# Cached keys of an encoder step: staged through a DRAM scratch into float32r tiles and transposed in that type

## Chip, cores and metric

The kernel runs on one core of a Trainium2 chip. The metric is the time of one execution on the device, in microseconds (us). TensorE (PE) multiplies matrices and transposes tiles; each of its products or transpositions is a pair of instructions, a weight load (listed as PEld) and a MATMUL that streams the other operand. VectorE (DVE), ScalarE (ACT) and GpSimd (POOL) do the rest of the arithmetic. SyncE (SP) issues the DMAs, in one queue and in order; 16 DMA engines carry them out.

## What is computed

One inference step of a four-layer encoder: 256 prompt tokens and 8 streams of 16 sample tokens, model width 2048, everything in float32. Every layer makes one projection of the normalised tokens, runs a token mixer with 12 heads beside a cross-attention with 4 heads into 256 memory tokens, multiplies both by a SiLU gate and projects back. Layers 0 and 3 use mixer A (sliding window), layer 1 mixer B (latent attention), layer 2 mixer C (chunk band). Cut to the attention with cached keys, for which the change matters:

```python
def attend(q, k, v, bias, valid, sink):
    ...
    s = jnp.einsum("bqhgd,bkhd->bhgqk", qg, k, ...) * (d ** -0.5)
    ...
    o = jnp.einsum("bhgqk,bkhd->bqhgd", p.astype(v.dtype), v)

# sample tokens, per stream: the cached rows stand ahead of the new ones
# A: cache_a_k, 128 rows, 4 heads of 128     C: cache_c_k, 512 rows, 12 heads of 128
# B: cache_b_ckv, 512 rows of 256, and cache_b_krope, 512 rows of 64
# cross-attention: cache_mem_k, 256 rows, 4 heads of 128, in every layer
```

The caches hold keys with one row per token, while a score product on TensorE needs the head's 128 dimensions on the partitions. So every 128x128 block of a cached key is transposed before it is used.

## The kernel before

The work is written in program order and a scheduler of the framework lays it out on the engines, so that products of the next projection fill the time between the steps of an attention. Memory keys and values of the prompt come first (`memory_kv`: 4 layers, two projections `pn_m` each), then the four layers. A layer projects (`proj_nat`, tiles `pn_...`, output columns 512 or 320 wide), mixes, makes the gate (`proj_tr`, `pt_g`, 384 columns wide) and projects back (`pt_o`; in the last layer `pn_o`). All these products run on weights that `w_split` loads from DRAM in pieces of 512 KB (`raw_...`, L144) and splits into two float32r halves: ScalarE rounds (`whi_...`), VectorE takes the rest (`wlo_...`). The pool `rawp` holds three such pieces. A second pool, `cchp`, holds five tiles of 512 KB for cached keys and values; while the memory keys are made, every other group of four rows of weight blocks uses it too (`ahead`).

A cached key is loaded straight from the input into a float32 tile of `cchp`: `kxs` for the memory keys (L450), `ak` for mixer A (L557), `kccs` for C (L711), `ckvkn` for the latent rows of B (L984); the rotary rows `krokn` (L986) go to a slot of `xtp`. `tr` (L101 to L103) transposes one block of 128 rows into a PSUM bank: the block is the weight operand, the identity `identr` streams past it. Four blocks fill a bank (`mkpsxs`, `mkpsp`, `ktpas`, `ktpcs`, `ctkn`, `krkn`), and VectorE or ScalarE copies it to SBUF (`kcT...`, `mkT...`, or the halves `chkn` and `clkn`). Banks of the kind `pt` are two, those of the kinds `s`, `o` and `ht` one each. The prompt's own memory keys take another way: they are written to a DRAM scratch (`memk_s`) and read back as `mk`.

One transposition in the kernel already works on float32r: line 1041 in `sample_b`, tile `rtbs`, 32 blocks of 64 columns.

Of the kernel before, what the change touches and what calls it, by code (L numbers as in the profile page):

```python
# [18 lines left out]
P = 128  # L19
# [40 lines left out]
def encoder_step(ctx: ExitStack, tc: tile.TileContext, ins: dict, outs: list, layers=(0, 1, 2, 3)):  # L60
# [25 lines left out]
    def cache_half(nm, q=2):  # L86
        return cchp.tile([P, q, 1024 // q], F32, tag="cch", name=nm)

    def mm(out, lhsT, rhs, start=True, stop=True):
        return nc.tensor.matmul(out, lhsT=lhsT, rhs=rhs, start=start, stop=stop)  # L90
# [43 lines left out]

    def w_split(nm, src, ncols, gcol=None, ahead=False):
# [24 lines left out]

    def proj_nat(nm, xt, w, ncols, ts=(0, 1, 2), gcol=None, first=0, ahead=False):
        nk = len(xt)
        ps = [pjb(f"pn_{nm}{t}") for t in ts]
        kstep = min(4, nk)
        order = [(first + i) % nk for i in range(0, nk, kstep)]
        for kg in order:
            wt = w_split(f"{nm}{kg}", w[kg * P:(kg + kstep) * P], ncols,
                         None if gcol is None else gcol[:, kg:kg + kstep], ahead and (kg // kstep) % 2 == 1)
            for i, t in enumerate(ts):
                for kk in range(kstep):  # L170
                    k = kg + kk
                    xh = xt[k][:, 0, t * P:(t + 1) * P]
                    xl = xt[k][:, 1, t * P:(t + 1) * P]
                    wh, wl = wt[kk]
                    mm(ps[i][:, :ncols], xh, wh, k == order[0], False)
                    mm(ps[i][:, :ncols], xh, wl, False, False)
                    mm(ps[i][:, :ncols], xl, wh, False, k == order[-1] + kstep - 1)
        return ps

    def proj_tr(nm, xt, w, first=0):  # L180
# [97 lines left out]
    def head_scale(n, f, g=None, nt=NT):  # L278
# [3 lines left out]
        if g is not None:  # L282
            nc.gpsimd.tensor_tensor(out=v, in0=v, in1=g.unsqueeze(1).to_broadcast([P, nh, HD]), op=ALU.mult)

    def memory_kv():
        xt = []
# [134 lines left out]
    def cross(l, xqT, oT, mul=False):  # L421
        mk, mv = cache_half(f"mk{l}"), cache_half(f"mv{l}")
        nc.sync.dma_start(out=mk, in_=memk_s[l].rearrange("(t p) d -> p t d", p=P))
        nc.sync.dma_start(out=mv, in_=memv_s[l].rearrange("(t p) d -> p t d", p=P))

        def kT(nm, mk):
            res = []
# [12 lines left out]

        mkT = kT(f"p{l}", mk)
        for h in range(4):
            attn_full(f"x{l}{h}", xqT[:, h, 0:256], mkT[h], mv[:, 0, h * P:(h + 1) * P],
                      mv[:, 1, h * P:(h + 1) * P], oT[:, H + h, 0:256], mul)
        for b2 in range(NB // 2):
            nm = f"xs{l}{b2}"
            mk, mv = ([cache_half(f"{t}{nm}{i}") for i in range(2)] for t in "kv")
            for t_, src in ((mk, "cache_mem_k"), (mv, "cache_mem_v")):
                for i in range(2):
                    nc.sync.dma_start(out=t_[i], in_=I[src][l, 2 * b2 + i].rearrange("(t p) h d -> p t (h d)", p=P))  # L450
            s = atb(f"s_{nm}", "s")
            for i in range(2):
                mkT = kT(f"{nm}{i}", mk[i])
                c0 = SP0 + DS * (2 * b2 + i)
# [96 lines left out]
    def sample_a(l, j, p2, qs, kT, vn, sink_r, oT):  # L551
        kvs = slice(2 * p2, 2 * p2 + 2)
        kcs, vcs = [], []
        for i in range(2):
            for ts, src in ((kcs, "cache_a_k"), (vcs, "cache_a_v")):
                ts.append(cache_half(f"a{src[-1]}{l}{p2}{i}", 4))
                nc.sync.dma_start(out=ts[i].rearrange("p b (h d) -> p b h d", h=2),  # L557
                                  in_=I[src][j, 4 * i:4 * i + 4, :, kvs, :].rearrange("b p h d -> p b h d"))
        for b2 in range(4):
            nm = f"as{l}{p2}{b2}"  # L560
            ps = atb(f"ktp{nm}", "s")
            for i in range(4):
                tr(ps[:, i * P:(i + 1) * P], kcs[b2 // 2][:, 2 * (b2 % 2) + i // 2, (i % 2) * P:(i % 2 + 1) * P])
            kcT = sm.tile([P, 512], F32, tag="kcT", name=f"kcT{nm}", bufs=4)
# [103 lines left out]
    def layer_c(l, xt, rx, xres, last):  # L668
# [3 lines left out]
        for g in range(3):  # L672
# [32 lines left out]
            for b in range(NB):  # L705
                nm = f"cs{g}{b}"
                kc, vc = [], []
                for ts, src in ((kc, "cache_c_k"), (vc, "cache_c_v")):
                    for i in range(2):
                        ts.append(cache_half(f"{src[-1]}c{nm}{i}"))  # L710
                        nc.sync.dma_start(out=ts[i], in_=I[src][0, b, 256 * i:256 * i + 256, hs, :].rearrange("(t p) h d -> p t (h d)", p=P))  # L711
# [57 lines left out]
    def layer_b(l, xt, rx, xres, last):  # L769
# [73 lines left out]
        def two_heads(qc):  # L843
# [137 lines left out]
        def key_norms(b):  # L981
            nm = f"kn{b}"
            raw = cache_half(f"ckv{nm}", 4)
            nc.sync.dma_start(out=raw, in_=I["cache_b_ckv"][0, b].rearrange("(t p) d -> p t d", p=P))  # L984
            kro = slot(f"kro{nm}")[:, 0:256].rearrange("p (t d) -> p t d", t=4)
            nc.sync.dma_start(out=kro, in_=I["cache_b_krope"][0, b].rearrange("(t p) d -> p t d", p=P))  # L986
            ss = tiny.tile([P, 48], F32, tag="kss", name=f"ss{nm}", bufs=2)
# [7 lines left out]
            for a in range(2):  # L995
                ps = atb(f"ct{nm}{a}", "ht")
                for kt in range(4):
                    tr(ps[:, kt * P:(kt + 1) * P], raw[:, kt, a * P:(a + 1) * P])
                nc.scalar.copy(ch[:, a, :], ps)
# [3 lines left out]
            for kt in range(4):  # L1003
                tr(ps[:64, kt * P:(kt + 1) * P], kro[:, kt, :])
            krT = sm.tile([P, 512], F32, tag="kcT", name=f"krT{nm}", bufs=4)
# [212 lines left out]

    setting = setup()
    memory_kv()  # L1220
    next(setting)
    xt = []
# [9 lines left out]
    for l in layers:  # L1232
        last = l == layers[-1]
        if l in (0, 3):
            xt, rx, xres = layer_a(l, l // 3, xt, rx, xres, last)
        elif l == 1:
            xt, rx, xres = layer_b(l, xt, rx, xres, last)
        else:
            xt, rx, xres = layer_c(l, xt, rx, xres, last)
# [33 lines left out]
```

## Time and profile before

| what | us |
|---|---|
| time before, median of 3 runs (2868.43 to 2872.82) | 2870.96 |
| the profiled execution, its own time | 2873.3 |
| its span, from the first to the last instruction | 2870.2 |
| PE busy | 2837.7 (99%) |
| PE weight loads busy | 2484.1 (87%) |
| VectorE busy | 1345.5 (47%) |
| ScalarE busy | 1322.9 (46%) |
| DMA engines busy | 47.6% of the span |

Durations of MATMULs overlap: the next begins before the end of the last has left the array. What one costs in a row of its kind is therefore the distance from its start to the start of the next, not its own duration; busy time is the union of the durations. "Idle before" is the time in which an engine had nothing running, with what ended it. The granted clock (PEclk) is a share of 2.4 GHz.

### The profile page before, as it was taken

What the parts mean: (1) busy time and instruction counts of PE and PEld (TensorE: products, weight loads), DVE (VectorE), ACT (ScalarE), POOL (GpSimd) and SP (SyncE); (2) the same over time, 40 slices, a digit from 0 to 9 for tenths busy, and PEclk for the clock granted to TensorE, in tenths of its full rate; (3) what the DMA queues carried; (4) which work ended last, traced back from release to release, by engine and by line L of the source; (5) the groups of instructions that cost most, each with busy time, mean ns of one, the idle gap of its engine ahead of it and who ended that gap; (6) DMA issues with size and microseconds to landing.
All of it is one profiled execution on the core that took longest, in us unless ns stands there. A gap on an engine that the chain in (4) does not pass through costs nothing.

```text
span 2870.2 us, 43881 instructions
## 1 busy us (share of the span) xinstructions
PE 2837.7 (99%) x17106; PEld 2484.1 (87%) x17106; DVE 1345.5 (47%) x2569; ACT 1322.9 (46%) x2819; POOL 425.7 (15%) x437
## 2 busy tenths in 40 slices
PE   8999999999999999999999999999999999999999
PEld 6867888999989987888898878788989988789987
DVE  5544345553435456565534434344545344445433
ACT  6655455443444366454434444444434344554332
POOL 1100111111100045333111101010101111011100
PEclk9999999999999999999999999999999999999999
DMA  7776453354444632000544465656566444533443
GB/s 255 249 264 211 158 173 117 125 186 152 143 138 118 191 92 73 16 19 26 162 161 139 138 199 193 222 178 239 180 233 230 151 136 132 195 114 100 133 157 128
DMA packets 314625, 446.79 MB, mean 156 GB/s; under 512 B 20629, under 2 KB 183462, under 8 KB 314418
## 3 DMA queue, kind: packets, MB, share of 16 engines
q1 hardware_dynamic: 314418, 444.00, 47.6%
q8 instruction: 134, 2.20, 0.3%
q14 instruction: 73, 0.60, 0.1%
HBM read 412.46 MB, written 34.69 MB: 156 GB/s over the span
## 4 chain that ended last, share of the span: by engine, by line
PE 96%; DMA 2%; DVE 1%; ACT 1%; SPq 0%; issue 0%; DVEq 0%; ACTq 0%
PE pt_g L90 19%; PE pt_o L90 14%; PE pn_aq L90 7%; PE kpkn L90 5%; PE pn_o L90 5%; PE pn_m L90 4%; PE pn_xq L90 4%; PE pn_cv L90 3%; PE pn_ck L90 3%; PE pn_cq L90 3%; PE pn_av L90 2%; PE pn_ak L90 2%; PE ktpcs L103 2%; PE s_bs L90 1%; PE pn_bqb L90 1%; PE pn_bq L90 1%
## 5 line engine op out<-in xcount | busy, mean ns | idle before, releaser
L90 PE MATMUL pt_g<-xt_x,whi_g 128*128 128x384 f32 x2048 | 532.4, 341 | 0.0
L90 PE MATMUL pt_o<-og,whi_o 128*128 128x384 f32 x1536 | 379.2, 334 | 0.0
L90 PEld LDWEIGHTS pt_g<-xt_x,whi_g 128*128 128x128 f32 x2048 | 367.3, 188 | 7.4 <-issue 4.9
L90 PE MATMUL pt_g<-xt_x,wlo_g 128*128 128x384 f32 x1024 | 342.9, 342 | 0.0
L150 DVE TENSOR_TENSOR wlo_o<-raw_o,whi_o 128x1024 fp32r<-128x1024 f32 x128 | 157.2, 1228 | 264.8 <-ACT whi_o L149 264.6
L90 PEld LDWEIGHTS pt_o<-og,whi_o 128*128 128x128 f32 x1536 | 276.1, 188 | 0.0
L149 ACT CAST whi_o<-raw_o 128x1024 fp32r<-128x1024 f32 x128 | 134.6, 1052 | 281.5 <-PE pt_o L90 147.5
L90 PE MATMUL pt_o<-og,wlo_o 128*128 128x384 f32 x768 | 245.7, 335 | 0.0
L150 DVE TENSOR_TENSOR wlo_g<-raw_g,whi_g 128x1024 fp32r<-128x1024 f32 x128 | 164.0, 1281 | 159.0 <-ACT whi_g L149 155.4
L149 ACT CAST whi_g<-raw_g 128x1024 fp32r<-128x1024 f32 x128 | 134.2, 1049 | 167.7 <-PE pt_g L90 142.9
L90 PEld LDWEIGHTS pt_g<-xt_x,wlo_g 128*128 128x128 f32 x1024 | 191.9, 188 | 5.4 <-issue 4.6
L90 PE MATMUL pn_aq<-whi_aq,xt_x 128*128 128x512 f32 x576 | 185.9, 398 | 0.0
L90 PE MATMUL pn_m<-whi_m,xt_m 128*128 128x512 f32 x512 | 161.6, 394 | 0.5 <-ACT whi_m L154 0.4
L90 PEld LDWEIGHTS pt_o<-og,wlo_o 128*128 128x128 f32 x768 | 143.2, 188 | 0.0
L90 PE MATMUL kpkn<-wk,chkn 128*128 128x384 f32 x512 | 133.7, 343 | 0.0
L155 DVE SCALAR_TENSOR_TENSOR wlo_m<-raw_m,gc_mem,whi_m 128x512 fp32r<-128x512 f32 x128 | 97.6, 804 | 75.7 <-ACT whi_m L154 75.7
L90 PEld LDWEIGHTS pn_aq<-whi_aq,xt_x 128*128 128x128 f32 x576 | 107.4, 188 | 22.5 <-issue 1.2
L90 PE MATMUL pn_xq<-whi_xq,xt_x 128*128 128x512 f32 x384 | 122.9, 397 | 0.5 <-ACT xt_x L214 0.5
L90 PE MATMUL pn_o<-whi_o,og 128*128 128x512 f32 x384 | 119.6, 391 | 0.0
L90 PE MATMUL pn_aq<-wlo_aq,xt_x 128*128 128x512 f32 x288 | 115.0, 401 | 0.0
L90 PEld LDWEIGHTS pn_m<-whi_m,xt_m 128*128 128x128 f32 x512 | 95.8, 189 | 21.2 <-ACT whi_m L154 1.1
L154 ACT ACTIVATE whi_m<-raw_m,gc_mem 128x512 fp32r<-128x512 f32 x128 | 85.8, 717 | 58.6 <-PE pn_m L90 58.2
(499 smaller groups left out, 5872.3 us busy)
## 6 DMA issues: line engine op xcount, KB each, us to landing
raw_o<-in_w_out_dram SPq DMA_DIRECT2D x128, 512.0 KB
raw_m<-in_w_mem_kv_dram SPq DMA_DIRECT2D x64, 512.0 KB
raw_g<-in_a_w_in_dram SPq DMA_DIRECT2D x64, 512.0 KB
raw_aq<-in_a_w_in_dram SPq DMA_DIRECT2D x48, 512.0 KB
kccs<-in_cache_c_k_dram SPq DMA_DIRECT2D x48, 512.0 KB
vccs<-in_cache_c_v_dram SPq DMA_DIRECT2D x48, 512.0 KB
kxs<-in_cache_mem_k_dram SPq DMA_DIRECT2D x32, 512.0 KB
vxs<-in_cache_mem_v_dram SPq DMA_DIRECT2D x32, 512.0 KB
```

The lines of the kernel that those rows point to most:

```text
L90: return nc.tensor.matmul(out, lhsT=lhsT, rhs=rhs, start=start, stop=stop)
L103: nc.tensor.transpose(out, in_, ident[:k, :k])
L149: nc.scalar.copy(hi[:, :, :ncols], r)
L150: nc.vector.tensor_tensor(lo[:, :, :ncols], r, hi[:, :, :ncols].bitcast(F32), ALU.subtract)
L154: nc.scalar.activation(hi[:, i, :ncols], r[:, i, :], AF.Copy, scale=g)
L155: nc.vector.scalar_tensor_tensor(lo[:, i, :ncols], r[:, i, :], g, hi[:, i, :ncols].bitcast(F32), ALU.mult, ALU.subtract)
```

## The change

Every cached key gets a second home in DRAM. `stage` makes a DRAM tile of the same shape as the later SBUF tile and puts the copy on a list; `move` takes copies from that list and issues them on SP, DRAM to DRAM, right behind a weight load (`issue_after`). `key_half` later loads the staged copy into a tile of `cchp` whose type is float32r (the DMA itself sees both sides as float32). `trr` transposes it with float32r on both sides of the transposition. The copies out of PSUM and the score products are untouched, and the cached values are loaded as before.

The copies are 104: 32 of memory keys, 8 of A, 48 of C, 8 of latent rows of B (512 KB each) and 8 of rotary rows (128 KB). Those for layer 0 are issued behind weight loads of `memory_kv` from its second layer on, those for layer 1's memory keys behind gate loads of layer 0, those for B, for C and for layer 2's memory keys behind gate loads of layer 1, the six `wkv` loads (four each) and the loads of rotary rows (three each), those for layer 3 behind gate loads of layer 2. The transpositions are 832: 384 `ktpcs`, 256 `mkpsxs`, 64 `ktpas`, 64 `ctkn`, 32 `krkn` and 32 `mkpsp`.

```diff
+    moves, staged = [], {}
+
+    def stage(key, view):
+        t_ = drp.tile(list(view.shape), F32, name="stg_" + "_".join(str(k) for k in key))
+        moves.append((t_, view))
+        staged[key] = t_ if len(view.shape) == 3 else t_.rearrange("p b h d -> p b (h d)")
+
+    def move(n, after=None):
+        for _ in range(min(n, len(moves))):
+            dst, view = moves.pop(0)
+            if after is None:
+                nc.sync.dma_start(out=dst, in_=view)
+            else:
+                with tc.issue_after(after.ins):
+                    nc.sync.dma_start(out=dst, in_=view)
+
+    def key_half(nm, key, q=2):
+        t_ = cchp.tile([P, q, 1024 // q], F32R, tag="cch", name=nm)
+        nc.sync.dma_start(out=t_.bitcast(F32), in_=staged.pop(key))
+        return t_
+
+    def trr(out, in_):
+        nc.tensor.transpose(out.bitcast(F32R), in_, identr)
+
...
-            nc.sync.dma_start(out=raw[:, :, :ncols], in_=src[hf:hf + q * P].rearrange("(k p) n -> p k n", p=P))
+            load = nc.sync.dma_start(out=raw[:, :, :ncols], in_=src[hf:hf + q * P].rearrange("(k p) n -> p k n", p=P))
+            move(moved, load)
...
-            wt = w_split(f"{nm}{kg}", w[kg * P:(kg + 4) * P], 256)
+            wt = w_split(f"{nm}{kg}", w[kg * P:(kg + 4) * P], 256, moved=1 if nm[0] == "g" else 0)
...
-                ps = proj_nat(f"m{l}{part}", xt, I["w_mem_kv"][l, :, part * 512:(part + 1) * 512], 512, (0, 1), gc, ahead=True)
+                ps = proj_nat(f"m{l}{part}", xt, I["w_mem_kv"][l, :, part * 512:(part + 1) * 512], 512, (0, 1), gc, ahead=True,
+                              moved=1 if l > 0 else 0)
...
-                        tr(ps[:, kt * P:(kt + 1) * P], kc[kt // 2][:, kt % 2, h * P:(h + 1) * P])
+                        trr(ps[:, kt * P:(kt + 1) * P], kc[kt // 2][:, kt % 2, h * P:(h + 1) * P])
...
-            nc.sync.dma_start(out=raw, in_=I["b_w_kv_b"][0, :, qc * 512:(qc + 1) * 512].rearrange("(a p) n -> p a n", p=P))
+            load = nc.sync.dma_start(out=raw, in_=I["b_w_kv_b"][0, :, qc * 512:(qc + 1) * 512].rearrange("(a p) n -> p a n", p=P))
+            move(4, load)
...
-            raw = cache_half(f"ckv{nm}", 4)
-            nc.sync.dma_start(out=raw, in_=I["cache_b_ckv"][0, b].rearrange("(t p) d -> p t d", p=P))
-            kro = slot(f"kro{nm}")[:, 0:256].rearrange("p (t d) -> p t d", t=4)
-            nc.sync.dma_start(out=kro, in_=I["cache_b_krope"][0, b].rearrange("(t p) d -> p t d", p=P))
+            rawr = key_half(f"ckv{nm}", ("b", b), 4)
+            raw = rawr.bitcast(F32)
+            kror = slot(f"kro{nm}", F32R)[:, 0:256].rearrange("p (t d) -> p t d", t=4)
+            kro = kror.bitcast(F32)
+            load = nc.sync.dma_start(out=kro, in_=staged.pop(("r", b)))
+            move(3, load)
...
+    stage_mem(0)
+    stage_a(0)
     memory_kv()
+    assert not moves
...
+        if l in (0, 2):
+            stage_mem(l + 1)
+        if l == 2:
+            stage_a(1)
...
+            for b in range(NB):
+                stage(("b", b), I["cache_b_ckv"][0, b].rearrange("(t p) d -> p t d", p=P))
+                stage(("r", b), I["cache_b_krope"][0, b].rearrange("(t p) d -> p t d", p=P))
+            stage_mem(2)
+            for g in range(3):
+                for b in range(NB):
+                    for i in range(2):
+                        stage(("c", g, b, i), I["cache_c_k"][0, b, 256 * i:256 * i + 256, 4 * g:4 * g + 4, :].rearrange("(t p) h d -> p t (h d)", p=P))
             xt, rx, xres = layer_b(l, xt, rx, xres, last)
+            move(len(moves))
```

On SP, in `memory_kv`, where the loads of the second layer's weights `raw_m` begin. Before:

```order
L144 DMA raw_m_519<-in_w_mem_kv_dram 128x2x512
L144 DMA raw_m_627<-in_w_mem_kv_dram 128x2x512
L144 DMA raw_m_675<-in_w_mem_kv_dram 128x2x512
L144 DMA raw_m_747<-in_w_mem_kv_dram 128x2x512
L144 DMA raw_m_635<-in_w_mem_kv_dram 128x2x512
```

The same place now:

```order
L170 DMA raw_m_531<-in_w_mem_kv_dram 128x2x512
L170 DMA raw_m_639<-in_w_mem_kv_dram 128x2x512
L105 DMA stg_m_0_110<-in_cache_mem_k_dram 256x1x512
L170 DMA raw_m_690<-in_w_mem_kv_dram 128x2x512
L105 DMA stg_m_3_113<-in_cache_mem_k_dram 256x1x512
L170 DMA raw_m_765<-in_w_mem_kv_dram 128x2x512
L105 DMA stg_m_6_116<-in_cache_mem_k_dram 256x1x512
```

Between the loads of this layer now stand copies of 512 KB (`stg_m`, `stg_a`), 12 in all.

On SP, in the gate of layer 1, with loads for the cross-attention (`kxs`, `vxs`) among the gate's weights `raw_g`. Before:

```order
L144 DMA raw_g_8743<-in_b_w_in_dram 128x4x256
L450 DMA kxs_8217<-in_cache_mem_k_dram 128x2x512
L144 DMA raw_g_8785<-in_b_w_in_dram 128x4x256
L450 DMA kxs_8218<-in_cache_mem_k_dram 128x2x512
L450 DMA vxs_8219<-in_cache_mem_v_dram 128x2x512
L450 DMA vxs_8220<-in_cache_mem_v_dram 128x2x512
L144 DMA raw_g_8815<-in_b_w_in_dram 128x4x256
```

The same place now:

```order
L170 DMA raw_g_8874<-in_b_w_in_dram 128x4x256
L105 DMA stg_m_3_7006<-in_cache_mem_k_dram 256x1x512
L109 DMA kxs_8337<-stg_m_4_1959 128x1024
L170 DMA raw_g_8917<-in_b_w_in_dram 128x4x256
L105 DMA stg_m_4_7007<-in_cache_mem_k_dram 256x1x512
L109 DMA kxs_8339<-stg_m_5_1960 128x1024
L487 DMA vxs_8341<-in_cache_mem_v_dram 128x2x512
L487 DMA vxs_8342<-in_cache_mem_v_dram 128x2x512
L170 DMA raw_g_8948<-in_b_w_in_dram 128x4x256
L105 DMA stg_m_5_7008<-in_cache_mem_k_dram 256x1x512
```

All 32 gate loads of this layer have a copy behind them, and the key loads read the scratch in whole rows of 1024 elements.

On PE, at a sample of mixer C (`ktpcs` are key blocks, `pt_cs` and `o_cs` transposed probabilities, `pn_cv` and `ht_ck` belong to the next group of heads). Before:

```order
L103 MATMUL ktpcs_16045<-identr,kccs_16022 128x128
L103 MATMUL pt_cs_15988<-identr,pr_cs_15978 128x128 x4
L103 MATMUL o_cs_15987<-identr,pr_cs_15978 128x128
L103 MATMUL ktpcs_16045<-identr,kccs_16022 128x128
L103 MATMUL ktpcs_16045<-identr,kccs_16024 128x128 x2
L103 MATMUL ktpcs_16052<-identr,kccs_16022 128x128 x2
L103 MATMUL ktpcs_16052<-identr,kccs_16024 128x128 x2
L90 MATMUL pn_cv_16874<-whi_cv_16932,xt_x_13814 128x512
```

The same place now:

```order
L113 MATMUL ktpcs_16241<-identr,kccs_16218 128x128 x2
L113 MATMUL ktpcs_16241<-identr,kccs_16220 128x128
L129 MATMUL pt_cs_16184<-identr,pr_cs_16174 128x128 x4
L129 MATMUL o_cs_16183<-identr,pr_cs_16174 128x128
L113 MATMUL ktpcs_16241<-identr,kccs_16220 128x128
L113 MATMUL ktpcs_16248<-identr,kccs_16218 128x128 x2
L113 MATMUL ktpcs_16248<-identr,kccs_16220 128x128 x2
L129 MATMUL ht_ck_17054<-identr,nat_ck_17008 128x128 x3
```

The blocks of a key stand in the same kind of runs between the same neighbours, a few instructions earlier or later. Counted over the whole order of PE, the 832 transpositions stand in 183 unbroken runs before and in 188 now; 140 of the runs, in both, are followed by a float32r product with 128 weight columns (`pt_g`, `pt_o`, `pn_...` or `kpkn`).

## Rows read from the trace of the kernel before

**Rows 1.** The page: PE's busy time, and the DMA queue with most traffic.

```profile
PE 2837.7 (99%) x17106; PEld 2484.1 (87%) x17106; DVE 1345.5 (47%) x2569; ACT 1322.9 (46%) x2819; POOL 425.7 (15%) x437
q1 hardware_dynamic: 314418, 444.00, 47.6%
```

**Rows 2.** Groups by form, PE and PEld: count, busy us, mean ns, idle before.

```profile
L103 PE MATMUL ktpcs<-identr,kccs 128*128 128x128 f32 x384 | 56.0, 274 | 1.2 <-DMA kccs<-in_cache_c_k_dram 1.1
L103 PE MATMUL krkn<-identr,krokn 128*64 128x128 f32 x32 | 4.8, 272 | 0.0
L1041 PE MATMUL rtbs<-identr,rhlbs 128*64 128x128 f32 x32 | 3.7, 237 | 0.0
...
L103 PEld LDWEIGHTS ktpcs<-identr,kccs 128*128 128x128 f32 x384 | 45.3, 141 | 10.9 <-issue 4.7 <-PE o_cs L90 0.8 <-PE snp L90 0.8
L103 PEld LDWEIGHTS krkn<-identr,krokn 128*64 128x64 f32 x32 | 3.5, 112 | 0.4
L1041 PEld LDWEIGHTS rtbs<-identr,rhlbs 128*64 128x64 f32 x32 | 2.8, 111 | 0.2
```

**Rows 3.** Timeline of PE at a sample of mixer C: start us, length us.

```profile
1758.48 0.93 PE L103 MATMUL ktpcs<-identr,kccs 128*128 128x128 f32 x7
1759.17 0.48 PE L90 MATMUL pn_cv<-whi_cv,xt_x 128*128 128x512 f32 x1
1759.48 0.40 PE L90 MATMUL pn_cv<-wlo_cv,xt_x 128*128 128x512 f32 x1
1759.72 0.27 PE L103 MATMUL ht_ck<-identr,nat_ck 128*128 128x128 f32 x1
```

**Rows 4.** Timeline of PE, then of PEld, around float32r transpositions of mixer B.

```profile
1186.25 0.51 PE L90 MATMUL kpkn<-wk,chkn 128*128 128x384 f32 x2
1186.60 0.34 PE L90 MATMUL kpkn<-wk,clkn 128*128 128x384 f32 x1
1186.78 0.40 PE L1041 MATMUL rtbs<-identr,rhlbs 128*64 128x128 f32 x4
1187.02 0.57 PE L90 MATMUL kpkn<-wk,chkn 128*128 128x384 f32 x2
1187.42 0.34 PE L90 MATMUL kpkn<-wk,clkn 128*128 128x384 f32 x1
...
1186.96 0.30 PEld L90 LDWEIGHTS kpkn<-wk,chkn 128*128 128x128 f32 x2
```

**Rows 5.** Waits, of all engines and of SP: us in total, times, longest.

```profile
DVE mkTxs L437 <- PE mkpsxs L103: 45.0, 24, 5.3
ACT kcTcs L720 <- PE ktpcs L103: 39.6, 27, 3.9
...
SPq L144 <- DVE wlo_m L155: 79.6, 45, 4.7
```

**Rows 6.** Busy by window; at the end granted clock, DMA share, GB/s.

```profile
40.00:85.00 45.00, 44.86 (x199) 36.82 (x198) 25.04 (x33) 27.72 (x55) 6.64 (x3) 1.00 0.71 237
843.00:1005.00 162.00, 160.90 (x1071) 150.44 (x1070) 70.61 (x102) 66.15 (x130) 5.02 (x2) 1.00 0.50 150
1734.00:2156.00 422.00, 420.78 (x3317) 353.91 (x3317) 190.83 (x387) 188.30 (x384) 45.91 (x57) 1.00 0.62 209
```

**Rows 7.** DMA queue and issues from 196 to 210 us: packets, MB, share.

```profile
q1 hardware_dynamic: 2339, 4.04, 87.0%
...
shear_cs<-bias_c SPq DMA_DIRECT2D x1, 838.5 KB
shear_c<-bias_c SPq DMA_DIRECT2D x1, 576.0 KB
```

**Rows 8.** Timeline: the gate's 21st load in layer 1, a PSUM copy, the load's use.

```profile
943.35 0.37 SPq L144 DMA_DIRECT2D raw_g<-in_b_w_in_dram  x1
...
959.25 0.58 ACT L435 COPY mkTxs<-mkpsxs 128x512 f32<-128x512 f32 x1
960.57 1.05 ACT L149 CAST whi_g<-raw_g 128x1024 fp32r<-128x1024 f32 x1 [0.73 <-ACT mkTxs L435]
```

More of the change, by code (lines that the diff above doesn't have):

```diff
@@ L132, in prompt_bias, with w_split @@
         return bm
-    def w_split(nm, src, ncols, gcol=None, ahead=False):
+    def w_split(nm, src, ncols, gcol=None, ahead=False, moved=0):
         res = []
@@ L159, in w_split, with proj_nat @@
         return res
-    def proj_nat(nm, xt, w, ncols, ts=(0, 1, 2), gcol=None, first=0, ahead=False):
+    def proj_nat(nm, xt, w, ncols, ts=(0, 1, 2), gcol=None, first=0, ahead=False, moved=0):
         nk = len(xt)
@@ L167, in proj_nat @@
             wt = w_split(f"{nm}{kg}", w[kg * P:(kg + kstep) * P], ncols,
-                         None if gcol is None else gcol[:, kg:kg + kstep], ahead and (kg // kstep) % 2 == 1)
+                         None if gcol is None else gcol[:, kg:kg + kstep], ahead and (kg // kstep) % 2 == 1, moved)
             for i, t in enumerate(ts):
@@ L283, in head_scale, with stage_mem, stage_a @@
             nc.gpsimd.tensor_tensor(out=v, in0=v, in1=g.unsqueeze(1).to_broadcast([P, nh, HD]), op=ALU.mult)
+    def stage_mem(l):
+        for b in range(NB):
+            stage(("m", l, b), I["cache_mem_k"][l, b].rearrange("(t p) h d -> p t (h d)", p=P))
+    def stage_a(j):
+        for p2 in range(2):
+            for i in range(2):
+                stage(("a", j, p2, i), I["cache_a_k"][j, 4 * i:4 * i + 4, :, 2 * p2:2 * p2 + 2, :].rearrange("b p h d -> p b h d"))
     def memory_kv():
@@ L421, in cross, with kT @@
     def cross(l, xqT, oT, mul=False):
-        mk, mv = cache_half(f"mk{l}"), cache_half(f"mv{l}")
-        nc.sync.dma_start(out=mk, in_=memk_s[l].rearrange("(t p) d -> p t d", p=P))
+        mk, mv = cchp.tile([P, 2, 512], F32R, tag="cch", name=f"mk{l}"), cache_half(f"mv{l}")
+        nc.sync.dma_start(out=mk.bitcast(F32), in_=memk_s[l].rearrange("(t p) d -> p t d", p=P))
         nc.sync.dma_start(out=mv, in_=memv_s[l].rearrange("(t p) d -> p t d", p=P))
-        def kT(nm, mk):
+        def kT(nm, mk, tr):
             res = []
@@ L439, in kT @@
             return res
-        mkT = kT(f"p{l}", mk)
+        mkT = kT(f"p{l}", mk, trr)
         for h in range(4):
@@ L446, in cross @@
             nm = f"xs{l}{b2}"
[L447 to L450, printed above, removed]
+            mk = [key_half(f"k{nm}{i}", ("m", l, 2 * b2 + i)) for i in range(2)]
+            mv = [cache_half(f"v{nm}{i}") for i in range(2)]
+            for i in range(2):
+                nc.sync.dma_start(out=mv[i], in_=I["cache_mem_v"][l, 2 * b2 + i].rearrange("(t p) h d -> p t (h d)", p=P))
             s = atb(f"s_{nm}", "s")
             for i in range(2):
-                mkT = kT(f"{nm}{i}", mk[i])
+                mkT = kT(f"{nm}{i}", mk[i], trr)
                 c0 = SP0 + DS * (2 * b2 + i)
@@ L554, in sample_a @@
         for i in range(2):
[L555 to L558, printed above, removed]
+            kcs.append(key_half(f"ak{l}{p2}{i}", ("a", j, p2, i), 4))
+            vcs.append(cache_half(f"av{l}{p2}{i}", 4))
+            nc.sync.dma_start(out=vcs[i].rearrange("p b (h d) -> p b h d", h=2),
+                              in_=I["cache_a_v"][j, 4 * i:4 * i + 4, :, kvs, :].rearrange("b p h d -> p b h d"))
         for b2 in range(4):
@@ L562, in sample_a @@
             for i in range(4):
-                tr(ps[:, i * P:(i + 1) * P], kcs[b2 // 2][:, 2 * (b2 % 2) + i // 2, (i % 2) * P:(i % 2 + 1) * P])
+                trr(ps[:, i * P:(i + 1) * P], kcs[b2 // 2][:, 2 * (b2 % 2) + i // 2, (i % 2) * P:(i % 2 + 1) * P])
             kcT = sm.tile([P, 512], F32, tag="kcT", name=f"kcT{nm}", bufs=4)
@@ L706, in layer_c @@
                 nm = f"cs{g}{b}"
[L707 to L711, printed above, removed]
+                kc = [key_half(f"kc{nm}{i}", ("c", g, b, i)) for i in range(2)]
+                vc = [cache_half(f"vc{nm}{i}") for i in range(2)]
+                for i in range(2):
+                    nc.sync.dma_start(out=vc[i], in_=I["cache_c_v"][0, b, 256 * i:256 * i + 256, hs, :].rearrange("(t p) h d -> p t (h d)", p=P))
                 s = atb(f"s_{nm}", "s")
@@ L997, in key_norms @@
                 for kt in range(4):
-                    tr(ps[:, kt * P:(kt + 1) * P], raw[:, kt, a * P:(a + 1) * P])
+                    trr(ps[:, kt * P:(kt + 1) * P], rawr[:, kt, a * P:(a + 1) * P])
                 nc.scalar.copy(ch[:, a, :], ps)
@@ L1003, in key_norms @@
             for kt in range(4):
-                tr(ps[:64, kt * P:(kt + 1) * P], kro[:, kt, :])
+                trr(ps[:64, kt * P:(kt + 1) * P], kror[:, kt, :])
             krT = sm.tile([P, 512], F32, tag="kcT", name=f"krT{nm}", bufs=4)
@@ L1236, in encoder_step @@
         elif l == 1:
+            for b in range(NB):
[3 more added lines that the diff above has]
+            for g in range(3):
+                for b in range(NB):
+                    for i in range(2):
+                        stage(("c", g, b, i), I["cache_c_k"][0, b, 256 * i:256 * i + 256, 4 * g:4 * g + 4, :].rearrange("(t p) h d -> p t (h d)", p=P))
             xt, rx, xres = layer_b(l, xt, rx, xres, last)
+            move(len(moves))
         else:
```

## The prediction

> **What bounds the kernel now.** I read the page's busy times first, then the groups by form for the transpositions, then the timeline around two of them, then the waits and the DMA shares. PE is busy for 2837.7 us of a span of 2870.2; the other compute engines stand at half of it or less, the DMA queue at 47.6% [rows 1]. So PE sets the end, and 32.5 us of idle time is all that it has. That holds in the stage with most of the touched work, too: over the samples of mixer C PE is busy for 420.78 of 422 us at the full clock (granted 1.00, the 2.4 GHz level) [rows 6], and before the 384 transpositions of cached C keys it sat idle for 1.2 us in all [rows 2]. VectorE and ScalarE wait for the transpositions, not the other way round: 45.0 us for the memory keys, 39.6 us for the C keys [rows 5]. What is taken from a transposition there comes off the path.
>
> **What a transposition costs before.** Its own duration misleads: 274 ns on average for the C keys [rows 2]. Seven in a row last 0.93 us from the first start to the last end; less the last one's 0.27 and divided by six, they start 0.110 us apart [rows 3]. The product behind them is listed early, at 1759.17, and is itself longer for it. But the one after it starts at 1759.48, that is 1.00 us after the first transposition; less one ordinary distance of such products (0.24, from 1759.48 to 1759.72) this leaves 0.76, again 0.109 a piece. So a run costs 0.11 us per block, and leaving it costs nothing extra.
>
> **What it costs after.** The kernel has one transposition in float32r already, with the same identity streaming past. It starts at 1186.78, the next product at 1187.02: four in 0.24 us, 0.060 apart; by duration, (0.40 - 0.24) / 3 gives 0.054 [rows 4, 2]. These have 64 weight columns, the changed ones (but for 32) 128. What does the width do? The weight load of the float32 form takes 112 ns at 64 columns and 141 at 128; in float32r at 64 it takes 111, so the type leaves the load alone and the width should add some 29 ns to it [rows 2]. In full on the path that gives 0.060 + 0.029, about 0.090 us a block; if the load lies wholly beside the stream of the block before, 0.054 to 0.060. I take 0.062, close to the lower end: in the float32 run a load of 141 ns goes with a distance of 110, so loads do run into each other and beside the streams. Both ends stay in the range.
>
> Leaving such a run does cost something. Behind the four, two `kpkn` products take from 1187.02 to 1187.42, 0.40 us, against 0.35 for two ordinary ones (1186.25 to 1186.60) [rows 4]. The reason is in the loads: two ordinary loads in a row are 0.11 us apart (0.30 less one length of 0.19) [rows 4], which a float32 transposition covers and a float32r one of 0.06 does not. So each run that is followed by a float32r product with 128 weight columns gives 0.05 us back. There are 140 such runs in the order of PE. Where a run ends at another transposition or a score product, I count nothing.
>
> **The sum.** 832 blocks by (0.110 - 0.062) is 39.9 us off; 140 exits by 0.05 is 7.0 us back. That leaves 32.9 us. The profiled execution took 2873.3 us, 2.3 above the median of the runs: 2840.4 by its own time, 2838.1 against the median. I add 2 us for new short waits, which no row prices: PE comes sooner to instructions that wait for the copies out of PSUM (bounds: nothing, and the PSUM rival below). That gives **2840 us**.
>
> The Trainium skill (TensorE: Matmul & The Clock Gate, section Back-to-back issue gap) speaks against so large a gain: it gives about 81 ns as the sustained distance for pairs of a weight load and a 128-column matmul. With 81 in place of 62 and an exit of about 0.03, the sum would be 24.1 - 4.2, some 20 us off: an estimate of 2851. The 0.060 of the `rtbs` rows disagrees with it at 64 columns; no run here shows 128. Its mechanism is the first rival below.
>
> **What it adds.** 104 copies of DRAM to DRAM, about 51 MB on top of 444 [rows 1]: 96 of 512 KB and 8 of 128 KB. What does a copied byte cost the DMA engines? The trace has such copies: from 196 to 210 us the shears of the bias, DRAM to DRAM, 838.5 and 576.0 KB, are over a third of the 4.04 MB moved at a share of 87.0%; that is 332 GB/s at a full share [rows 7]. The stretch from 40 to 85 us, with nothing but loads and stores, gives 237 / 0.71, or 334 [rows 6]. So a copied byte costs as much as a loaded one, and a piece of 512 KB takes 1.6 us of all 16 engines. 51 MB take about 154 us, 5% of the span, which lifts the mean share from 48 to 53%. What matters is where.
>
> The tightest place is `memory_kv`: 12 copies (19 us) within about 45 us at a share of 0.71 [rows 6] make 32 + 19 = 51 us of work in 45. The 6 us too much have cover: weight loads there wait for their buffers (79.6 us in 45 waits [rows 5]), since up to eight pieces are ahead of PE. They land later and still in time, and after the twelfth copy the backlog drains. Without that cover they would cost their 6 us. The second place is the gate of layer 1: 32 copies in 162 us at a share of 0.50 [rows 6] make 81 + 51 = 132 of 162. The 21st load there was issued at 943.35 and first read at 960.57 [rows 8], so 17 us of lead stand against a copy ahead in the queue of 1.6 us. The other copies go beside work with less traffic. On SP a copy waits for nothing but its turn, as its scratch tile is used once; what is queued behind it is the next weight load, held up by less than 1 us of issuing (0.37 us for a load [rows 8]). A key load waits for its copy, which was issued a layer earlier. So I cost the copies at nothing.
>
> **Rivals.** *The weight load paces the block.* At 128 columns the distance is 0.090. Then 832 by 0.020 is 16.6 us off, exits cost 0.02 each, 2.8 us in all: 13.8 off, 2857 us. For it: 141 against 111 ns of load. Against it: the overlap of loads in float32 runs. *The copies out of PSUM pace the runs.* A bank of four blocks takes ScalarE 0.58 us to copy [rows 8], and PE would fill it in 0.25; there are two banks of `pt` and one of each other kind. If half of the gain turns into waits there, 2855 us. For it: up to eight blocks stand in a run. Against it: PE had other products to do between the runs in every stage, and they are still there. *The type does nothing at 128 columns.* Then 0.11 stays and the time is 2871, give or take a few us. Against it: `krkn` and `rtbs` have the same shape and differ in type alone, 4.8 against 3.7 us for 32 [rows 2]. *The DMA engines become the bound in layer 1's gate.* Each of its 32 steps takes 162 / 32 = 5.1 us and already uses 2.5 of DMA. If a copy took 2.6 us or more (read and write counted twice, say), the gate would follow the DMA; from 3.6 us a step loses 1 us, 32 us in all, and the gain is gone. At 4 us a piece it ends at about 2885, slower than before. Against it: the price of 1.6 us from the shears.
>
> **How the numbers follow.** Forecast as worked out, 2828 to 2850: 0.68. Its lower end is a distance of 0.058 without any exit (43 us off), its upper end the forecast with 10 us of DMA or PSUM waits. Paced by the load, 2857: 0.13. Paced by PSUM, 2855: 0.09. No difference: 0.05. DMA-bound and slower: 0.05. A range from 2828 to 2858 holds the first three cases, 0.90 less what falls off at the edges. About 0.2%, or 5.7 us, can be told from no change; the first three cases are beyond it: faster 0.90, same 0.05, slower 0.05.
>
> **What would show it.** Right: the `ktpcs` group about 45% shorter in busy time, seven in a row 0.06 apart, weight loads of 140 ns; products behind a run 0.05 late; PE's idle time still near 32 us; a DMA share near 0.53 and no wait of PE for `kccs`, `kxs` or weights beyond a few us. Wrong: a distance near 0.09 with loads of 140 (load-paced), idle time before `ktpcs` and `s_cs` in the samples (PSUM), waits of ScalarE's `whi_m` or `whi_g` on DMA between 40 and 100 or 843 and 1005 us (copies).

## The result

The change makes the kernel faster: 2855.8 us (median of 4 runs, 2853.3 to 2856.4) against 2869.7 us (4 runs), a ratio of 0.9950 with a 95% interval of 0.9933 to 0.9967. Measured a second time, beside the later experiments, it took 2853.7 us against 2872.6, ratio 0.9931 (0.9919 to 0.9944). By the medians it takes off 14 and 19 us. The forecast was 2840, that is 30 to 33 us off: the sign was right, and the time lies inside the range, which was drawn wide enough to hold a rival at 2857, but about half of the gain did not come.

The page of the changed kernel, PE and the busiest DMA queue, against [rows 1]:

```profile
span 2854.5 us, 43990 instructions
PE 2821.7 (99%) x17106; PEld 2469.0 (86%) x17106; DVE 1340.2 (47%) x2569; ACT 1322.2 (46%) x2819; POOL 429.7 (15%) x437
q1 hardware_dynamic: 329394, 495.39, 52.9%
```

PE is still the bound. Its busy time fell by 16.0 us and its idle time hardly moved: 2854.5 - 2821.7 = 32.8 us, against 32.5. So what is missing did not turn into waits on PE; the work on PE itself shrank by less than forecast. The groups by form (count, busy us, mean ns, idle before), against [rows 2]:

```profile
L113 PE MATMUL ktpcs<-identr,kccs 128*128 128x128 f32 x384 | 45.2, 245 | 0.0
L113 PE MATMUL krkn<-identr,krokn 128*64 128x128 f32 x32 | 3.3, 226 | 0.0
L1080 PE MATMUL rtbs<-identr,rhlbs 128*64 128x128 f32 x32 | 3.3, 224 | 0.0
...
L113 PEld LDWEIGHTS ktpcs<-identr,kccs 128*128 128x128 f32 x384 | 40.9, 140 | 11.3 <-issue 2.2 <-PE o_cs L116 2.2 <-PE snp L116 1.7
L113 PEld LDWEIGHTS krkn<-identr,krokn 128*64 128x64 f32 x32 | 2.7, 111 | 0.4
```

The busy time of the C keys' group went from 56.0 to 45.2 us, 19% and not the 45% of the forecast. The group with 64 weight columns, `krkn`, came down from 4.8 to 3.3 us and now stands where `rtbs` of the same shape stands in the same trace (226 against 224 ns): for 64 columns the reading of the forecast was right. The loads kept their durations, 140 and 111 ns.

The timeline of PE around two runs of C keys (start us, length us), against [rows 3]:

```profile
1783.18 0.80 PE L113 MATMUL ktpcs<-identr,kccs 128*128 128x128 f32 x8
1783.82 0.46 PE L116 MATMUL pn_cq<-whi_cq,xt_x 128*128 128x512 f32 x1
1784.12 0.39 PE L116 MATMUL pn_cq<-wlo_cq,xt_x 128*128 128x512 f32 x1
...
1796.76 0.45 PE L113 MATMUL ktpcs<-identr,kccs 128*128 128x128 f32 x4
1797.04 0.47 PE L116 MATMUL pn_cq<-wlo_cq,xt_x 128*128 128x512 f32 x1
1797.35 0.39 PE L116 MATMUL pn_cq<-whi_cq,xt_x 128*128 128x512 f32 x1
```

Reckoned as the prediction reckoned before: the second product starts 0.94 us after the start of the run of eight and 0.59 after that of the run of four; less one ordinary distance of 0.24 this leaves 0.70 and 0.35, 0.0875 a block with its share of the exit, where 0.109 stood and the forecast wanted 0.062 and 0.05 for each exit (0.55 and 0.30). Over the whole trace, counted on PEld from each weight load to the next one of any kind, the 832 transpositions take 85.4 us (85.3 in the second profile of this kernel) where they took 101.1: 15.7 less, where the forecast had 39.9 for the blocks.

The second thing to see is in the memory phase. In the waits of the changed kernel (us in total, times, longest) there is a line that the kernel before does not have:

```profile
ACT whi_m L181 <- DMA raw_m<-in_w_mem_kv_dram: 7.8, 4, 4.0
```

And the windows, against [rows 6] (span of the window, busy by engine, at the end clock, DMA share, GB/s):

```profile
40.00:85.00 45.00, 44.87 (x199) 36.83 (x198) 25.03 (x33) 27.60 (x56) 6.63 (x3) 1.00 0.96 338
95.00:100.00 5.00, 4.49 (x20) 3.38 (x18) 3.14 (x3) 2.26 (x4) 4.41 (x2) 1.00 0.57 210
843.00:1005.00 162.00, 160.92 (x1076) 150.54 (x1076) 72.10 (x104) 67.72 (x132) 5.03 (x2) 1.00 0.75 236
```

From 40 to 85 us the DMA engines went from a share of 0.71 to 0.96. PE did not lose anything in that stretch. ScalarE did wait: one of the four waits (0.4 us, at 11.5 us) lies ahead of the first copy, the others end at 74.05 (2.6 us), 85.74 (0.9) and 121.62 (4.0). Between the last two the DMA engines had caught up: from 95 to 100 us their share is 0.57. The load that the longest wait was for was issued only at 115.52, the first of its kind since 109.13; on SP stood, in order:

```profile
109.13 0.53 SPq L170 DMA_DIRECT2D raw_m<-in_w_mem_kv_dram  x1
109.71 4.08 SPq L154 DMA_DIRECT2D bma<-shear_a  x2
115.52 0.38 SPq L170 DMA_DIRECT2D raw_m<-in_w_mem_kv_dram  x1
```

SP waited there 2.7 us for a shear of the bias (`shear_a`) to land and 1.7 us for an earlier weight load. In the kernel before, both shears stand behind 35 loads `raw_m` in SP's order, now behind 37 and 38. How much of this wait is the copies' backlog and how much the new order was not tried. In layer 1's gate (843 to 1005 us) the share is 0.75 and PE as busy as before.

### The profile page after: what moved, and what is told of

Read it like the earlier page. It is cut to its first block, busy times and chain, and to the rows that moved or that the text cites. A ratio compares the mean times of both kernels' runs of the same rounds, so it can differ in the third digit from the quotient of the medians.

```text
span 2854.5 us, 43990 instructions
## 1 busy us (share of the span) xinstructions
PE 2821.7 (99%) x17106; PEld 2469.0 (86%) x17106; DVE 1340.2 (47%) x2569; ACT 1322.2 (46%) x2819; POOL 429.7 (15%) x437
## 4 chain that ended last, share of the span: by engine, by line
PE 96%; DMA 2%; DVE 1%; ACT 1%; SPq 0%; issue 0%; ACTq 0%; DVEq 0%
PE pt_g L116 19%; PE pt_o L116 14%; PE pn_aq L116 7%; PE kpkn L116 5%; PE pn_o L116 5%; PE pn_xq L116 4%; PE pn_m L116 4%; PE pn_cq L116 4%; PE pn_cv L116 4%; PE pn_ck L116 3%; PE pn_av L116 2%; PE pn_ak L116 2%; PE s_bs L116 1%; PE pn_bqb L116 1%; PE pn_bq L116 1%; PE ktpcs L113 1%
```

## Experiments

The question is where half of the gain went. Theory 1: to the float32r block itself, which costs 0.085 us at 128 weight columns since its weight load paces it. Rivals: the stream or the write of the result paces it; or the copies took the gain.

**What a block costs by itself.** A probe leaves the computation out and runs rows of transpositions and products. Its core, with `...` where lines are left out:

```diff
+    def row(nm, f, n=24):
+        out = bank(nm)
+        for i in range(n):
+            f(out, i)
+        fill(8)
...
+    for real in (True, False):
+        t = "r" if real else "f"
+        for w in (32, 64, 96, 128):
+            row(f"t{t}_{WIDTH[w]}", lambda o, i: tr(o, i, w, P, real))
+        for w in (64, 128):
+            row(f"t{t}half_{WIDTH[w]}", lambda o, i: tr(o, i, w, 64, real))
```

Here `fill` issues float32r products of 512 columns into the tile `sink`, and `real` chooses float32r or float32.

> This kernel leaves the whole computation out and runs only rows of transpositions and products on resident tiles: 24 alike in a row, then mixes of 1 to 8 transpositions followed by two float32r products of 384 columns. Theory 1, the weight load paces a float32r transposition: the distance from start to start goes with the weight columns at 128 streamed columns, about 0.045 us at 32, 0.058 at 64, 0.072 at 96 and 0.085 at 128, and stays at 0.085 for 128 weight columns when only 64 columns stream past. Rival, the stream or the write of the result paces it: 128 weight columns with 64 streamed columns take half as long, about 0.045, and 32 to 96 weight columns at 128 streamed ones are no shorter than 0.06. For float32 the first expects 0.110 to fall to about 0.085 with 64 streamed columns, since the load of 128 columns stays; the rival expects 0.055. On leaving a run: by the first the price of a float32r run lies in the next ordinary weight load (about 0.108 after the last block instead of 0.085), so a run of three float32r blocks and one float32 block costs about 0.365 in all against 0.379 for four float32r ones and 0.44 for four float32 ones; if the price is one of changing the type, the mixed run is no cheaper than the pure one.

The timeline of PE: rows of 24, each followed by the products `sink`. The names end in a letter for the weight columns (a 32, b 64, c 96, d 128); `tr` is float32r, `tf` float32, `half` has 64 rows and so 64 streamed columns, `prod_d_d` is an ordinary product of 128 by 128.

```profile
37.09 1.60 PE L44 MATMUL tr_a<-identr,kr 128*32 128x128 f32 x24
38.52 2.08 PE L36 MATMUL sink<-kr 128*128 128x512 f32 x8
40.44 1.60 PE L44 MATMUL tr_b<-identr,kr 128*64 128x128 f32 x24
41.87 2.06 PE L36 MATMUL sink<-kr 128*128 128x512 f32 x8
43.77 1.82 PE L44 MATMUL tr_c<-identr,kr 128*96 128x128 f32 x24
45.42 2.06 PE L36 MATMUL sink<-kr 128*128 128x512 f32 x8
47.32 2.16 PE L44 MATMUL tr_d<-identr,kr 128*128 128x128 f32 x24
49.32 2.08 PE L36 MATMUL sink<-kr 128*128 128x512 f32 x8
...
54.80 2.19 PE L44 MATMUL trhalf_d<-identr,kr 64*128 64x64 f32 x24
56.91 2.11 PE L36 MATMUL sink<-kr 128*128 128x512 f32 x8
...
72.26 2.78 PE L46 MATMUL tf_d<-identr,kf 128*128 128x128 f32 x24
74.80 2.07 PE L36 MATMUL sink<-kr 128*128 128x512 f32 x8
...
80.29 1.72 PE L46 MATMUL tfhalf_d<-identr,kf 64*128 64x64 f32 x24
81.94 2.12 PE L36 MATMUL sink<-kr 128*128 128x512 f32 x8
...
103.59 2.79 PE L36 MATMUL prod_d_d<-kr 128*128 128x128 f32 x24
106.21 2.08 PE L36 MATMUL sink<-kr 128*128 128x512 f32 x8
```

From a row's start to the start of `sink`, divided by 24: float32r takes 0.060 us at 32 and at 64 weight columns, 0.069 at 96 and 0.083 at 128 (0.085 from load start to load start, from the second load of the row on). With 64 streamed columns and 128 weight columns it is 0.088, not less. So at 96 columns and above the width of the weights sets the distance, and the length of the stream does not: as theory 1 had it, and the rival of the stream falls. Two of theory 1's numbers missed. There is a floor of 0.060, where it had 0.045 at 32 columns. And float32, 0.106 at every width, fell to 0.069 with 64 streamed columns, where it had 0.085. So a float32 block goes with the length of its stream (in a transposition also the number of its rows), and its load of 128 columns needs less room than a float32r one, though both are listed with 140 ns. What the 128 columns do beyond being loaded (they are also 128 partitions of the result) the probe does not tell apart, so that it is the load that paces the block is not shown.

The mixed runs, six in a row, each of four transpositions and two products of 384 columns (here the first transposition of the first run, and the `sink` behind the sixth):

```profile
137.39 0.46 PE L44 MATMUL mix_rrrr<-identr,kr 128*128 128x128 f32 x4
141.69 1.98 PE L36 MATMUL sink<-kr 128*128 128x512 f32 x8
143.51 0.60 PE L46 MATMUL mix_ffff<-identr,kf 128*128 128x128 f32 x4
148.24 2.02 PE L36 MATMUL sink<-kr 128*128 128x512 f32 x8
150.10 0.38 PE L44 MATMUL mix_rrrf<-identr,kr 128*128 128x128 f32 x3
...
154.28 2.00 PE L36 MATMUL sink<-kr 128*128 128x512 f32 x8
```

A run of four float32r blocks costs 4.30 / 6 = 0.717 us, of four float32 ones 0.788: 0.072 less. Four blocks by (0.109 - 0.085) would be 0.096, so leaving the run gives 0.024 back. Three float32r blocks and a float32 one cost 0.697: the price of leaving goes when a float32 block stands last, so it is not one of changing the type. Two more mixes of the same probe agree: with the float32 block first the run costs 0.736, and with the types in turn, a float32 block last, 0.697. With products of 64 weight columns behind it, the pure float32r run was the cheapest (0.667 against 0.695), which agrees: a narrow load needs no cover.

**Pairs and single blocks.** A second probe:

```diff
+    for w, nm in ((72, "h"), (80, "i"), (112, "j")):
+        row(f"tr_{nm}", lambda o, i: tr(o, i, w, P, True))
...
+    for kinds in ("rs", "rf", "rp", "rq", "fp", "fq", "sp"):
+        out = bank(f"pair_{kinds}")
+        for i in range(24):
+            for c in kinds:
+                KIND[c](out, i)
+        fill(8)
...
+    for kinds in ("r", "f", "rr", "ff", "rrrr", "ffff", "rrrf"):
+        runs(kinds, 6)
```

> A second kernel that leaves the whole computation out and runs only rows on resident tiles: float32r transpositions of 72, 80 and 112 weight columns; 24 alternating pairs (r: float32r of 128 weight columns, s: float32r of 64, f: float32 of 128, p and q: float32r products of 128 and 64 weight columns with 128 streamed ones); and runs of r and f ahead of three products of 512 streamed columns. Theory 1 (each float32r transposition costs what its own weight load costs and leaves the next to pay for itself): 0.060 to 0.078 us at 72 to 112 columns; pairs of r and s 0.085 + 0.060 = 0.145, r and p 0.085 + 0.108 = 0.193, r and f 0.085 + 0.085 = 0.17, as in the mixed runs before. Theory 3 (the price belongs to the block that comes next, which must be loaded while r streams): r and s 0.145 too, but r and q no more than 0.06 + 0.085, and f and p clearly under f's 0.108 + p's 0.108, since a float32 stream hides the load of p: about 0.17. Ahead of products of 512 columns both expect one r and one f to cost the same within 0.01, and four r 0.07 less than four f; a single r that costs 0.08 more than a single f, as the kernel's traces seem to say, would speak against the probe as a picture of the kernel.

```profile
36.84 1.64 PE L44 MATMUL tr_h<-identr,kr 128*72 128x128 f32 x24
38.31 2.07 PE L36 MATMUL sink<-kr 128*128 128x512 f32 x8
40.22 1.64 PE L44 MATMUL tr_i<-identr,kr 128*80 128x128 f32 x24
41.70 2.06 PE L36 MATMUL sink<-kr 128*128 128x512 f32 x8
43.59 1.99 PE L44 MATMUL tr_j<-identr,kr 128*112 128x128 f32 x24
45.42 2.08 PE L36 MATMUL sink<-kr 128*128 128x512 f32 x8
47.34 3.52 PE L44 MATMUL pair_rs<-identr,kr 128*128 128x128 f32 x48
50.70 2.05 PE L36 MATMUL sink<-kr 128*128 128x512 f32 x8
```

The floor of 0.061 holds to 80 columns; 112 take 0.076. A pair of r and s takes 3.36 / 24 = 0.140, r and f 0.168: both as theory 1 had them (the first as theory 3 had it, too). But r and p take 0.214 instead of 0.193, r and q 0.161 instead of 0.145, f and p 0.196 instead of theory 3's 0.17 or the plain sum of 0.217. So neither theory is exact when an ordinary product follows: it costs some 0.02 more behind a float32r transposition than behind its own kind. Ahead of products of 512 columns, from the first of six runs to the last, one r and one f cost the same (0.808 and 0.807 a period), four r 1.060, four f 1.131, three r and one f 1.040: again 0.071 and 0.020. So a single block gains nothing. The kernel agrees: between products of 384 columns a single key block takes 0.286 us from its start to that of the second product, before (at 601.65 us) and in the changed kernel (at 2185.81). The 0.08 that the expectation mentions comes of blocks behind a float32 block: the first float32r start is listed 0.03 us after the block ahead (at 1955.50), a float32 start 0.11 after it (at 2092.67 before), so a run counted from its first start looks longer.

**What the copies cost.** The copies and the loads from the scratch alone, with float32 tiles (the prompt's memory keys and the rotary rows go back to float32 in the same way):

```diff
-        t_ = cchp.tile([P, q, 1024 // q], F32R, tag="cch", name=nm)
-        nc.sync.dma_start(out=t_.bitcast(F32), in_=staged.pop(key))
+        t_ = cchp.tile([P, q, 1024 // q], F32, tag="cch", name=nm)
+        nc.sync.dma_start(out=t_, in_=staged.pop(key))
...
-        nc.tensor.transpose(out.bitcast(F32R), in_, identr)
+        nc.tensor.transpose(out, in_, ident)
...
```

> All 104 copies and the loads from the scratch as in the changed kernel, but float32 tiles and float32 transpositions: what the copies cost alone. Theory 1 (the copies cost 3 us, all of it in the memory phase): 2869.7 + 3, about 2872.5, with ScalarE waiting for late weight loads between 90 and 125 us and nowhere else. Rival A (the copies cost nothing, as predicted, and the lost 3 us come from another order of the memory phase): 2869.7 within 1 us. Rival B (the copies cost more, spread over all layers, and that is where the missing 17 us went): 2880 or more.

Measured: 2873.1 us against 2872.5, ratio 1.0002 (0.9993 to 1.0011), that is -2 to +3 us. The time alone does not separate 3 us from nothing, and is nearer to rival A's nothing; rival B, 8 us and more, is out. The trace places a cost: ScalarE waits for raw weights in the memory phase, the line

```profile
ACT whi_m L181 <- DMA raw_m<-in_w_mem_kv_dram: 5.9, 4, 2.7
```

and the 768 products `pn_m`, each counted from its weight load to the next, take 180.6 us against 179.0 before. In all, the four profiles with the twelve crowded copies (this run, the changed kernel twice, and the run with float32 blocks last, below) have 180.6 to 182.7 us, and the four with none or two of them (before, and three runs below) 178.0 to 180.1: 2.4 us apart in the mean. So the copies cost some 2 us in the memory phase by the trace, which the whole time is too coarse to show. In layer 1's gate PE is busy for 160.92 of 162 us in the changed kernel, 160.90 before: the 32 copies there cost nothing.

The other side, the changed kernel with 5 copies of the 104, one for each kind of key, which every load of that kind reads:

```diff
-        t_ = drp.tile(list(view.shape), F32, name="stg_" + "_".join(str(k) for k in key))
-        moves.append((t_, view))
+        if key[0] not in kinds:
+            kinds[key[0]] = drp.tile(list(view.shape), F32, name="stg_" + "_".join(str(k) for k in key))
+            moves.append((kinds[key[0]], view))
+        t_ = kinds[key[0]]
```

> The changed kernel with 5 copies instead of 104: each kind of key (memory, A, latent, rotary, C) has one scratch tile, and every key load of that kind reads it, so 99 copies are left out and the attention sees wrong cached keys; loads, types and transpositions are those of the changed kernel. Theory 1: about 2853, 3 us less than the changed kernel, with the memory phase as before the change. Rival A: 2855.8. Rival B (copies took most of the missing gain): 2840 to 2845.

2852.1 us, ratio 0.9931 (0.9918 to 0.9943). The wait of ScalarE for raw weights is gone but for 0.1 us, and `pn_m` takes 179.2 us. The repeat of the changed kernel has 2853.7 us and the same ratio, 0.9931, so theory 1's 3 us are not seen in the time; against rival B, 2840 to 2845, it shows that the missing gain is not in the copies.

The same 12 early copies, spread out:

```diff
-            move(moved, load)
+            due[0] += moved
+            move(int(due[0] + 1e-6), load)
+            due[0] -= int(due[0] + 1e-6)
...
-                              moved=1 if l > 0 else 0)
+                              moved=1 / 6 if l > 0 else 0)
...
+        ps = proj_nat(f"av{l}", xt, w[:, 2048:2560], 512, moved=1 / 2 if l == 0 else 0)
```

> The changed kernel with the 12 copies for layer 0 spread out: the eight of memory keys go behind every sixth weight load of the memory phase from its second layer on (instead of one behind every load), the four of mixer A behind every second value load of layer 0. Theory 1 (crowded copies delay the weight loads): the 3 us come back, 2852.5 to 2853.5, and ScalarE's wait of 7.8 us for raw weights in the memory phase goes. Rival A (the copies are not the cause): 2855.8, unchanged. Rival C (the DMA engines have no room there, however the copies are placed): the same 3 us are lost later in the phase, 2855.8 with a wait between 130 and 230 us.

2855.1 us, ratio 0.9937 (0.9923 to 0.9950): no gain. The wait for `raw_m` fell from 7.8 to 0.2 us and `memory_kv` ended 3.6 us sooner, but the loss came back behind it, in layer 0's first projection:

```profile
ACT whi_xq L178 <- DMA raw_xq<-in_a_w_in_dram: 13.6, 3, 5.2
```

In the changed kernel this wait is 1.2 us. PE's first transposition of a memory key of the samples starts at 253.24 us, against 252.08 in the changed kernel: the 3.6 us are gone by then. That is rival C, in this one profile.

**The same kernel again, and two versions that follow from the above.** The repeat of the changed kernel gave the second ratio above.

> The changed kernel once more, on the same chip as the three beside it, so that they can be compared with it directly. All theories: 0.995 of the time before.

The last block of each bank in float32, from the same tile (the calls for C, memory keys, A and latent rows say which block is the last):

```diff
-    def trr(out, in_):
-        nc.tensor.transpose(out.bitcast(F32R), in_, identr)
+    def trr(out, in_, last=False):
+        if last:
+            nc.tensor.transpose(out, in_.bitcast(F32), ident)
+        else:
+            nc.tensor.transpose(out.bitcast(F32R), in_, identr)
...
```

> The changed kernel, but the last of the four blocks of each bank (C, memory keys, A, latent rows; not the rotary rows of 64 columns) goes through PE as float32, from the same tile. Theory 1 (the price of a float32r run is the load that comes behind it; a float32 block hides that load, and a float32 load behind a float32r block is cheap, as the probe's mixed runs of four say: 0.697 against 0.717 us): some 150 runs by 0.020, 3 us less than the changed kernel. Rival (each change of type costs, and the probe's runs do not carry over): 200 more float32 blocks by 0.025, 5 us more.

2858.1 us, ratio 0.9942 (0.9929 to 0.9956): no gain, and by the medians 4 us more than the repeat, where theory 1 had 3 us less and the rival 5 us more. The time is the rival's. In the runs of transpositions themselves theory 1 holds. A run of eight C keys, as above:

```profile
1786.68 0.37 PE L116 MATMUL ktpcs<-identr,kccs 128*128 128x128 f32 x3
1786.89 0.30 PE L114 MATMUL ktpcs<-identr,kccs 128*128 128x128 f32 x1
1786.94 0.46 PE L116 MATMUL ktpcs<-identr,kccs 128*128 128x128 f32 x3
1787.23 0.30 PE L114 MATMUL ktpcs<-identr,kccs 128*128 128x128 f32 x1
1787.29 0.48 PE L119 MATMUL pn_cq<-wlo_cq,xt_x 128*128 128x512 f32 x1
1787.60 0.63 PE L119 MATMUL pn_cq<-whi_cq,xt_x 128*128 128x512 f32 x2
```

The second product starts 0.92 us after the start of the run, 0.02 sooner than in the changed kernel. But the scheduler laid out the rest of the program differently: counted from weight load to weight load, the touched blocks take 4 us less than in the repeat, while gate products, `o_xs`, `s_cs` and others take 8 us more. Whether those 8 us come from the order or from the change of type was not tried, so the rival stands for the kernel as a whole.

No copy before 250 us (the copies for layer 0 are issued inside that layer):

```diff
+            plain = l == 0 and b2 < 2
+            if plain:
+                mk = [cache_half(f"k{nm}{i}") for i in range(2)]
...
+                if plain and b2:
+                    move(2, load)
...
```

> The changed kernel without any copy before 250 us: the memory keys of four of the eight streams of layer 0 are loaded straight from the input and transposed in float32 (32 blocks), the other four streams' keys are copied behind value loads inside layer 0, mixer A's behind weight loads of that layer. Theory 2 (until about 230 us the DMA engines have no room, wherever in that stretch the copies stand): the 3 us of the memory phase come back, less 0.7 us for 32 float32 blocks, so 2 to 2.5 us less than the changed kernel. Rival (the 3 us of the run with few copies came from the loads that read one tile, or from chance): no difference.

2853.0 us, ratio 0.9930 (0.9917 to 0.9942), 0.7 us less than the repeat: less than the 2 to 2.5 expected and inside the spread of the runs. Its trace has no wait for `raw_m` above 0.1 us. Both together:

> The last block of each bank in float32 and no copy before 250 us, together. By theories 1 and 2: 5 us less than the changed kernel, about 0.993 of the time before. By the rivals: 5 us more than it.

2854.4 us, ratio 0.9934 (0.9921 to 0.9946): neither the 5 us less of the theories nor the 5 us more of the rivals. No version is measurably faster than the changed kernel.

## Why the prediction was right and wrong

**PE bounds the kernel, and a block's saving comes off the path: right.** Idle time stayed at 32.8 us, and PE's busy time and the span fell by the same 16 us (16.0 and 15.7).

**A float32 block costs 0.11: right.** In the probe it is 0.106 by the row, 0.109 from load start to load start.

**A float32r block costs 0.062: wrong, and this is the step that failed.** It costs 0.085. By 832 blocks that is 19.1 us of the 39.9 forecast. The forecast had the 0.060 of `rtbs` right, but that is a floor that the probes show up to 80 weight columns. It had the width's price in hand, 29 ns of load, and took it for hidden because the loads of a float32 run overlap. They do overlap in the changed kernel too (140 ns long, about 0.085 apart); what counts is how soon the next can start. A row that was already there said more: two ordinary loads of 128 columns start 0.11 apart [rows 4], which gave no ground to expect 0.06 of a load of that width. The distance lies near the upper bound that the text named, 0.090.

**The rival "the weight load paces the block" had the right cause, as far as it was tested.** The distance follows the weight columns and not the stream. That the load itself is what holds the next block back is not shown: a float32 load of 128 columns is listed with the same 140 ns and lets a block follow in 0.069. The rival's time of 2857 is 1 us from the first measurement and 3 from the second. It was given 0.13, on the argument of overlapping loads.

The Trainium skill (TensorE: Matmul & The Clock Gate, section Back-to-back issue gap) says that the distance of such pairs is set by load and product together, and gives about 81 ns at 128 columns. The probe agrees within 5 ns for a transposition of 128 weight columns; at 64 it shows 60. For an ordinary float32r product of 128 by 128 it shows 109, 28 ns more than the section gives.

**Leaving a run costs 0.05: too much.** The probe has 0.024, which gives 140 x 0.026 = 3.6 us back to the gain. The place fits: a float32 block at the end of the run or a narrow load behind it takes the price away.

**The copies cost nothing: wrong by some 2 us, in the memory phase.** The mean share (0.53) was right, and so was layer 1's gate. In the memory phase the backlog of 6 us was to be hidden by the loads' lead and then to drain. It did drain, by 95 us, but the lead did not cover it: ScalarE waited twice before that. The longest wait came later, behind loads of the bias in SP's order. The forecast had added up DMA time from 40 to 85 us alone and had not followed the queue.

**Two us for PSUM waits: not seen.** PE's idle time rose by 0.3 us, and no run shows this term.

**The sum again**, with the measured terms: 832 x 0.024 = 20.0 off, 140 x 0.024 = 3.4 back, about 2 back for the copies: 14.6 us. The two measurements say 13.9 and 18.9, and differ by more than either of the smaller terms: they bear out the cost of a block, not those terms.

## What to carry over

A distance read at one width is not a law for another: look for the row of the same width, even of another operation. Loads that overlap can still pace a run, so read the distance from load start to load start, not whether they overlap. And DMA time that is added to a queue shifts what stands behind it in order: follow the queue past the crowded stretch, not only the share inside it.

## What was not expected of the hardware

- At the full clock (granted 1.00 in both probes) a float32r transposition has a floor of 0.060 us a block at 32 to 80 weight columns and then rises to 0.069 (96), 0.076 (112) and 0.083 to 0.085 (128), while the listed load lasts 140 ns at 128 in both types.
- A float32 transposition costs 0.106 to 0.109 at every width from 32 to 128, and 0.069 at 128 weight columns with 64 streamed columns, where float32r takes 0.088.
- Ordinary float32r products with 128 weight columns are 0.109 apart whether 64 or 128 columns stream past, 0.025 more than transpositions with the same load; with 64 weight columns they are 0.060 apart. Why the two differ stays open.
- In a run of four ahead of products of 384 columns, a float32 block in last place makes the run 0.020 us shorter than four float32r blocks, one in first place 0.019 longer.
